# Five rows beside the first decoding, a token shift on two engines, twelve buffers for the first modulation weights

## The chip, the cores and the metric

The kernel runs on one core of one Trainium2 chip. A core has five engines with a queue each: PE (TensorE, matrix products), DVE (VectorE), ACT (ScalarE), POOL (GpSimd) and SP (SyncE, which here only issues transfers). The metric is the device time of one execution in microseconds.

## The reference, cut to what matters

Two layers over 256 context tokens and 256 latent tokens of width 1024. Layer 0 mixes tokens by a bidirectional mLSTM, layer 1 by a bidirectional RWKV-7; behind each stands PEER, which retrieves 128 experts a token (8 heads, the best 16 of 256 candidates each).

```python
for i in range(DEPTH):
    mx = jnp.split((s_lat @ ada_w[i] + ada_b[i])[:, None, :], N_MOD, axis=-1)      # modulation
    mc = jnp.split((s_ctx @ ada_w[i] + ada_b[i])[None, None, :], N_MOD, axis=-1)
    hx = x * (1.0 + mx[1]) + mx[0]
    hc = ctx * (1.0 + mc[1]) + mc[0]
    ...
    x = _layernorm(DN_ALPHA * x + mx[2] * yx, ln_g[i, 0], ln_b[i, 0])
    hx = x * (1.0 + mx[4]) + mx[3]
    ...

# RWKV-7: token shift, then the projections of the six mixes
xm = h[None] + (shifted - h)[None] * mu[:, None, None, :]
r, k, v = jnp.einsum('nbtd,nde->nbte', xm[:3], w_rkv)
... xm[3] -> w1, w2 (decay), xm[4] -> a1, a2, xm[5] -> g1, g2

# PEER: ids of the experts, then a row of u and a row of v for each
u = jnp.take(u_tab, eidx, axis=0)
act = jax.nn.gelu(jnp.einsum('ted,td->te', u, xb), approximate=False)
wgt = gate * act
return jnp.einsum('te,ted->td', wgt, jnp.take(v_tab, eidx, axis=0))
```

## The kernel before, in words

Every fp32 product is made of three TensorE products of a hi and a lo part (`mm3`, L97 to L99). A weight is loaded (`load_raw`, L83 to L90), ScalarE copies it to its hi part (L77), and VectorE, or GpSimd where the caller says so, subtracts that to get the lo part (`split`, L78). TensorE thus waits in turn for a load, for ScalarE and for VectorE. A tile scheduler with a heap of priorities fixes the order of the instructions on every engine's queue when the kernel is built; an instruction that waits holds up all that stands behind it on its engine.

**The start.** `build` opens the weight stream (`open_w`, four raw buffers) and runs `ada_pass` for the first third of layer 0's modulation. It loads 16 tiles of 128 x 1024 from `ada_w`, in eight steps of two (L87), and TensorE multiplies each as it comes (L151). The tiles go into the four buffers of the weight stream, because the pass is called without buffers of its own. Then VectorE adds the bias (L156), TensorE transposes, and the modulation stands in columns. `mlstm` follows: it loads the tokens (`xT`, two transfers of 1 MB at L291, s = 0 for the context and s = 1 for the latents), modulates them in eight blocks (L299 on VectorE for one half, L297 on ScalarE for the other), makes the hi parts on ScalarE (L300) and the lo parts on VectorE (L301), and begins with the products for q and k. The space of `cw`, the weights of the convolution, is the one that the pass held before.

**The RWKV projections.** `rwkv_proj` makes six mixes. `mix(m, seqs)` builds, for each of eight blocks `kt`, a tile `xm` (three buffers) of both sequences or the latents alone: `h * om` (om is 1 − mu), plus the shifted `h` times `mu` (L667, VectorE), a hi part (L669, ScalarE) and a lo part. The first mix (for k) has `first=True`: its mult is on ScalarE (L653) and its lo part on VectorE for three blocks of four. The five others have the mult on VectorE (L655) and the lo part on GpSimd (L670):

```python
for s in seqs:
    if first:
        S.activation(xm[:, s], hk[s][:, kt, :], AF.Copy, scale=om[:, m, kt:kt + 1])
    else:
        V.tensor_scalar(xm[:, s], hk[s][:, kt, :], om[:, m, kt:kt + 1], None, op0=ALU.mult)
...
(V if first and kt % 4 < 3 else G).tensor_tensor(lo[:, kt, :], xf, hi[:, kt, :].bitcast(F32), op=ALU.subtract)
```

In order: k with its mix, the second mix `xw` (for the decay) called behind the second of eight k rows, the mix for r behind the fifth, then `xa`, the eight r rows (`r_ps`), `xv`, and the products for a (`lo_ps`), `xg` and v. The tiles hi and lo of a mix of both sequences have two buffers.

**The first decoding.** `peer_two` computes rows of the expert products (u rows) for 384 of the 512 tokens densely; for the last 128 tokens it gathers single rows by GpSimd (L1588), with a dot product on VectorE for each (L1596). `retrieval` finds the experts and decodes their ids (L1360 to L1370, all on VectorE). While it does, `between` puts work beside it: 12 u rows with lo parts on GpSimd, a modulation pass, and three more u rows into banks b3 to b5 whose results wait until slot C exists (L1631). Then u rows and gathers are interleaved.

## Time and profile before

| | |
|---|---|
| median of 3 runs | 3297.94 us (3294.22 to 3300.07) |
| the profiled execution | 3297.34 us, span of its instructions 3295.5 us |
| mean granted TensorE clock | 0.967 |
| TensorE busy | 3053.1 us, 93% of the span |
| VectorE busy | 2495.4 us, 76% |
| ScalarE busy | 1542.7 us, 47% |
| GpSimd busy | 766.9 us, 23% |

An engine's share is a mean over stages with different limits. It says little of what a change in one stage is worth; for that a stretch is looked at by itself, with the busy time of all engines and with what ended each wait. "Idle before" in a row is the time that the engine stood still ahead of the instruction, and the arrow names what ended it. Times that begin a row are counted from the start of the span.

### The profile page before, as it was taken

What the parts mean: (1) busy time and instruction counts of PE and PEld (TensorE: products, weight loads), DVE (VectorE), ACT (ScalarE), POOL (GpSimd) and SP (SyncE); (2) the same over time, 40 slices, a digit from 0 to 9 for tenths busy, and PEclk for the clock granted to TensorE, in tenths of its full rate; (3) what the DMA queues carried; (4) which work ended last, traced back from release to release, by engine and by line L of the source; (5) the groups of instructions that cost most, each with busy time, mean ns of one, the idle gap of its engine ahead of it and who ended that gap; (6) DMA issues with size and microseconds to landing.
All of it is one profiled execution on the core that took longest, in us unless ns stands there. A gap on an engine that the chain in (4) does not pass through costs nothing.

```text
span 3295.5 us, 54703 instructions
## 1 busy us (share of the span) xinstructions
PE 3053.1 (93%) x20325; PEld 2616.2 (79%) x20325; DVE 2495.4 (76%) x5426; ACT 1542.7 (47%) x2867; POOL 766.9 (23%) x672
## 2 busy tenths in 40 slices
PE   7999999799999899999997897788889999999998
PEld 4776799699988789877874764477879999888887
DVE  5838679767978788899788738996776939887555
ACT  3524343335733333465444447466644443444443
POOL 1110044331033333403342320011306830000000
PEclk8999999999999999999998999789999999999999
DMA  5236542686377788836884248575744554556554
GB/s 209 93 97 201 194 146 83 212 280 222 113 239 274 239 270 287 290 133 233 287 284 148 96 142 248 163 214 159 220 161 151 176 179 155 173 173 223 189 190 147
DMA packets 251883, 633.83 MB, mean 192 GB/s; under 512 B 39840, under 2 KB 97312, under 8 KB 251360
## 3 DMA queue, kind: packets, MB, share of 16 engines
q1 hardware_dynamic: 180672, 478.27, 44.1%
q0 software_dynamic: 37152, 135.28, 12.3%
q10 hardware_dynamic: 33792, 16.78, 1.8%
q8 instruction: 159, 2.61, 0.3%
q14 instruction: 108, 0.88, 0.1%
HBM read 589.06 MB, written 41.19 MB: 191 GB/s over the span
## 4 chain that ended last, share of the span: by engine, by line
PE 68%; DVE 17%; DMA 7%; issue 5%; ACT 2%; POOL 2%; SPq 0%; ACTq 0%; DVEq 0%; POOLq 0%
PE acc L1715 12%; PE acc L1820 11%; PE u_ps L97 7%; PE u_ps L99 7%; PE u_ps L98 7%; PE gp L1673 2%; PE ada_ps L151 2%; DMA unit<-urows,rows 1%; DVE lo_w L78 1%; DVE o_qk L327 1%; DMA raw<-ada_w 1%; DVE eq L1369 1%; DMA unit<-uT 1%; DVE xm L667 1%; PE vo L99 1%
## 5 line engine op out<-in xcount | busy, mean ns | idle before, releaser
L77 ACT ACTIVATE hi_w<-raw 128x1024 fp32r<-128x1024 f32 x339 | 358.1, 1057 | 504.4 <-PE u_ps L98 208.6
L78 DVE TENSOR_TENSOR lo_w<-raw,hi_w 128x1024 fp32r<-128x1024 f32 x281 | 345.8, 1231 | 277.2 <-ACT hi_w L77 277.1
L77 ACT ACTIVATE hi_w<-unit 128x512 fp32r<-128x512 f32 x522 | 326.3, 629 | 488.6 <-PE u_ps L98 263.4
L78 DVE TENSOR_TENSOR lo_w<-unit,hi_w 128x512 fp32r<-128x512 f32 x492 | 335.6, 691 | 150.0 <-ACT hi_w L77 148.6
L99 PE MATMUL u_ps<-hd,lo_w 128*128 128x384 f32 (+1 forms) x1024 | 345.5, 337 | 12.8 <-DVE lo_w L78 7.1
L97 PE MATMUL u_ps<-hd,hi_w 128*128 128x384 f32 (+1 forms) x1024 | 348.3, 340 | 2.1 <-ACT hi_w L77 1.0
L98 PE MATMUL u_ps<-hd,hi_w 128*128 128x384 f32 (+1 forms) x1024 | 344.3, 336 | 0.0
L99 PE MATMUL u_ps<-carry,lo_w 128*128 128x256 f32 x1088 | 307.4, 283 | 6.4 <-POOL lo_w L78 5.9
L97 PE MATMUL u_ps<-carry,hi_w 128*128 128x256 f32 x1088 | 309.1, 284 | 4.4 <-ACT carry L211 4.4
L98 PE MATMUL u_ps<-carry,hi_w 128*128 128x256 f32 x1088 | 307.0, 282 | 0.0
L1715 PE MATMUL acc<-lo_w,wh 128*128 128x512 f32 x718 | 283.7, 395 | 7.5 <-DVE lo_w L78 7.4
L1715 PE MATMUL acc<-hi_w,wh 128*128 128x512 f32 x718 | 282.9, 400 | 6.5 <-ACT hi_w L77 4.3
L1715 PE MATMUL acc<-hi_w,wl 128*128 128x512 f32 x718 | 282.1, 393 | 0.0
L1588 POOL DMA_INDIRECT unit<-vtab,rows x128 | 178.5, 1394 | 363.9 <-DVE xt L1601 181.6
L1588 POOL DMA_INDIRECT unit<-urows,rows x128 | 160.5, 1254 | 421.3 <-DVE unit L1596 271.2
L99 PEld LDWEIGHTS u_ps<-carry,lo_w 128*128 128x128 f32 x1088 | 206.4, 190 | 7.4 <-POOL lo_w L78 6.8
L97 PEld LDWEIGHTS u_ps<-carry,hi_w 128*128 128x128 f32 x1088 | 206.6, 190 | 5.4 <-ACT carry L211 4.8
L99 PEld LDWEIGHTS u_ps<-hd,lo_w 128*128 128x128 f32 x1024 | 195.7, 191 | 17.4 <-DVE lo_w L78 10.7
L98 PEld LDWEIGHTS u_ps<-carry,hi_w 128*128 128x128 f32 x1088 | 206.6, 190 | 0.8 <-DVE carry L212 0.2
L97 PEld LDWEIGHTS u_ps<-hd,hi_w 128*128 128x128 f32 x1024 | 195.9, 191 | 4.5 <-ACT hi_w L77 2.2
L98 PEld LDWEIGHTS u_ps<-hd,hi_w 128*128 128x128 f32 x1024 | 195.7, 191 | 1.1
L1596 DVE SCALAR_TENSOR_TENSOR unit<-unit,xt 128x1024 f32<-128x1024 f32 x128 | 155.0, 1219 | 36.0 <-DMA unit<-urows,rows 35.4
(526 smaller groups left out, 7551.7 us busy)
## 6 DMA issues: line engine op xcount, KB each, us to landing
raw<-vtab SPq DMA_DIRECT2D x144, 512.0 KB
unit<-uT SPq DMA_DIRECT2D x136, 512.0 KB
unit<-vtab SPq DMA_DIRECT2D x128, 512.0 KB
raw<-uT SPq DMA_DIRECT2D x128, 512.0 KB
raw<-ada_w SPq DMA_DIRECT2D x80, 512.0 KB
PK<-dr_pk SPq DMA_DIRECT2D x64, 448.0 KB
raw<-w_qkT SPq DMA_DIRECT2D x16, 512.0 KB
raw<-w_in SPq DMA_DIRECT2D x16, 512.0 KB
```

Source lines behind the costliest of these rows:

```text
L77: nc.scalar.activation(hi, raw, AF.Copy)
L78: (eng or nc.vector).tensor_tensor(lo, raw, hi.bitcast(F32), op=ALU.subtract)
L97: mm(out, lhi, rhi, start=start, stop=False)
L98: mm(out, lhi, rlo, start=False, stop=False)
L99: mm(out, llo, rhi, start=False, stop=stop)
L151: nc.tensor.matmul(ps[32 * g:32 * g + 32, :], E.sc[:, kt, :], raws[g // 2][:, g % 2 * 512:g % 2 * 512 + 512], start=kt == 0, stop=kt == KT ...
L327: V.scalar_tensor_tensor(dst, src, cw[:, ct, k:k + 1], dst, op0=ALU.mult, op1=ALU.add)
L1588: G.indirect_dma_start(out=t, out_offset=None, in_=src, in_offset=bass.IndirectOffsetOnAxis(ap=rows1[:, s:s + 1], axis=0))
L1596: return V.scalar_tensor_tensor(t, t, 1.0, xt, op0=ALU.mult, op1=ALU.mult, accum_out=act[:, s:s + 1])
L1673: mm(gp[:, t], At[t], Bg[:, x, t // 2, :, t % 2], start=x == 0, stop=x == 1)
L1715: mm(accs[2 * tt + n], l[:, ts], r, start=j == 0 and y == 0, stop=j == 127 and y == 2)
L1820: mm(acc[tt * 2 + n], l[:, x, ts], r[:, n * 512:(n + 1) * 512], start=(j + x == 0 and l is wh and r is vhi), stop=(j + x == 127 and l is wl))
```

## The change

Three edits. The first modulation pass gets 12 buffers of its own, in its own pool. In `mix`, the mult is on ScalarE and the lo part on VectorE for every mix. In `between`, five u rows instead of three stand beside the decoding; the two more are in the two banks of `ps_u`, and the rows that are left for later start two further on.

```diff
-        def mix(m, seqs, first=False):
+        def mix(m, seqs):
...
                 for s in seqs:
-                    if first:
-                        S.activation(xm[:, s], hk[s][:, kt, :], AF.Copy, scale=om[:, m, kt:kt + 1])
-                    else:
-                        V.tensor_scalar(xm[:, s], hk[s][:, kt, :], om[:, m, kt:kt + 1], None, op0=ALU.mult)
+                    S.activation(xm[:, s], hk[s][:, kt, :], AF.Copy, scale=om[:, m, kt:kt + 1])
...
                 S.activation(hi[:, kt, :], xf, AF.Copy)
-                (V if first and kt % 4 < 3 else G).tensor_tensor(lo[:, kt, :], xf, hi[:, kt, :].bitcast(F32),
-                                                                 op=ALU.subtract)
+                V.tensor_tensor(lo[:, kt, :], xf, hi[:, kt, :].bitcast(F32), op=ALU.subtract)
...
-        xk = mix(1, (0, 1), True)
+        xk = mix(1, (0, 1))
...
-                for x in range(3):
-                    beside.append((EARLY + LATER + x, ps.tile([128, TD], F32, name="u_ps", tag=f"b{3 + x}", bufs=1)))
-                    u_prod(beside[x][1], halves(load(uT[beside[x][0]]), G))
+                for x in range(5):
+                    up = ps_u.tile([128, TD], F32, name="u_ps") if x > 2 else \
+                        ps.tile([128, TD], F32, name="u_ps", tag=f"b{3 + x}", bufs=1)
+                    beside.append((EARLY + LATER + x, up))
+                    u_prod(up, halves(load(uT[EARLY + LATER + x]), G))
...
-                advance(ada_pass(E, A, 0, 0, m0, pool, ps, "ada", 2), None)
+                advance(ada_pass(E, A, 0, 0, m0, pool, ps, "ada", 2, own=12), None)
```

What the scheduler makes of it is seen at three places. The first is SP at the start of the program (`raw` is a weight tile, `xT_243` holds the context tokens and `xT_244` the latents, `cw` to `bg` are small tables). Before:

```order
L87 DMA raw<-ada_w 128x1024 x4
L291 DMA xT_243<-tokT 128x2048
L141 DMA ada_bt<-ada_b 2x512 x4
L87 DMA raw<-ada_w 128x1024 x12
L85 DMA raw<-w_gP 128x1024
L291 DMA xT_244<-tokT 128x2048
L263 DMA cw<-conv_wT 128x144
L265 DMA cb<-conv_bT 128x16
L267 DMA bq<-b_qkT 128x16
L269 DMA bg<-b_gT 128x1
L85 DMA raw<-w_qkT 128x1024 x4
```

And now:

```order
L87 DMA raw<-ada_w 128x1024 x5
L141 DMA ada_bt<-ada_b 2x512 x4
L87 DMA raw<-ada_w 128x1024 x11
L85 DMA raw<-w_gP 128x1024
L291 DMA xT_243<-tokT 128x2048
L263 DMA cw<-conv_wT 128x144
L265 DMA cb<-conv_bT 128x16
L267 DMA bq<-b_qkT 128x16
L269 DMA bg<-b_gT 128x1
L291 DMA xT_244<-tokT 128x2048
L85 DMA raw<-w_qkT 128x1024 x4
```

Both loads of xT moved behind the weights of the modulation, and xT_244 behind cw and the three small tables.

The second is VectorE where the second mix begins (`carry_18007` and `carry_18008` are the modulated tokens of the context and of the latents). Before:

```order
L670 TENSOR_TENSOR xlo<-xm,xhi 128x512
L667 SCALAR_TENSOR_TENSOR xm<-carry_18008,rmu,xm 128x192
L655 TENSOR_SCALAR xm<-carry_18007,rom 128x256
L655 TENSOR_SCALAR xm<-carry_18008,rom 128x256
L667 SCALAR_TENSOR_TENSOR xm<-carry_18007,rmu,xm 128x255
L667 SCALAR_TENSOR_TENSOR xm<-carry_18008,rmu,xm 128x4x63
```

And now (L664 is the old L667, and L667 the lo part, the old L670):

```order
L667 TENSOR_TENSOR xlo<-xm,xhi 128x512 x2
L664 SCALAR_TENSOR_TENSOR xm<-carry_18008,rmu,xm 128x192
L664 SCALAR_TENSOR_TENSOR xm<-carry_18007,rmu,xm 128x255
L664 SCALAR_TENSOR_TENSOR xm<-carry_18008,rmu,xm 128x4x63
L664 SCALAR_TENSOR_TENSOR xm<-carry_18007,rmu,xm 128x255
L667 TENSOR_TENSOR xlo<-xm,xhi 128x512 x2
```

The mults have left the queue, and a lo part stands in it for each block.

The third is GpSimd at the end of the first decoding (`unit` is the ring of buffers that loads and gathers share, `urows` the table of u rows). Before:

```order
L78 TENSOR_TENSOR lo_w<-unit,hi_w 128x512 x20
L1588 DMA unit<-urows,rows_3194 128x1024 x2
L78 TENSOR_TENSOR lo_w<-unit,hi_w 128x512 x2
L1588 DMA unit<-urows,rows_3194 128x1024
L78 TENSOR_TENSOR lo_w<-unit,hi_w 128x512 x4
L1588 DMA unit<-urows,rows_3194 128x1024 x123
```

And now (L1586 is the old L1588):

```order
L78 TENSOR_TENSOR lo_w<-unit,hi_w 128x512 x20
L1586 DMA unit<-urows,rows_3194 128x1024
L78 TENSOR_TENSOR lo_w<-unit,hi_w 128x512 x2
L1586 DMA unit<-urows,rows_3194 128x1024
L78 TENSOR_TENSOR lo_w<-unit,hi_w 128x512 x4
L1586 DMA unit<-urows,rows_3194 128x1024
L78 TENSOR_TENSOR lo_w<-unit,hi_w 128x512 x4
L1586 DMA unit<-urows,rows_3194 128x1024 x123
```

One gather fewer stands ahead of the first two lo parts, and four lo parts more stand among the first gathers. The order of TensorE is the same at this place.

## Rows read from the trace of the kernel before

**Rows 1.** The page: the chain that ended last, share of the span by engine.

```profile
PE 68%; DVE 17%; DMA 7%; issue 5%; ACT 2%; POOL 2%; SPq 0%; ACTq 0%; DVEq 0%; POOLq 0%
```

**Rows 2.** Busy time by stretch: length, each engine's us (instructions), granted clock, DMA share, GB/s.

```profile
60.00:150.00 90.00, 84.14 (x360) 66.80 (x359) 88.14 (x191) 57.90 (x74) 15.44 (x8) 1.00 0.27 87
...
1782.00:1802.00 20.00, 9.23 (x44) 7.02 (x43) 20.00 (x34) 9.81 (x15) 11.37 (x9) 0.76 0.00 0
1802.00:1841.00 39.00, 39.00 (x184) 32.57 (x184) 20.68 (x35) 15.18 (x26) 7.64 (x9) 0.95 0.30 95
1841.00:1888.00 47.00, 35.56 (x228) 33.13 (x227) 43.94 (x70) 23.95 (x38) 26.14 (x16) 0.89 0.29 91
1888.00:1912.00 24.00, 24.00 (x108) 19.81 (x107) 11.68 (x15) 8.21 (x15) 6.67 (x8) 1.00 0.33 107
```

The engines stand in the order PE, PEld (its weight loads), DVE, ACT, POOL.

**Rows 3.** The chain that ended last, 0 to 60 us: start, us, what.

```profile
1.74 3.68 DMA raw<-ada_w
```

**Rows 4.** TensorE's weight loads, first and fourth tile of ada_w: start, us, what [idle before].

```profile
5.53 0.22 PEld L151 LDWEIGHTS ada_ps<-raw,sc_lhs 128*32 128x32 f32 x4 [5.53 <-issue]
...
9.63 0.19 PEld L151 LDWEIGHTS ada_ps<-raw,sc_lhs 128*32 128x32 f32 x4 [1.10 <-DMA raw<-ada_w]
```

**Rows 5.** Timeline of all engines, end of the modulation pass and start of mlstm.

```profile
32.90 1.05 PE L151 MATMUL ada_ps<-raw,sc_lhs 128*32 128x512 f32 x4 [2.21 <-DMA raw<-ada_w]
...
35.95 0.33 SPq L263 DMA_DIRECT2D cw<-conv_wT  x1
...
37.75 1.85 SPq L85 DMA_DIRECT2D raw<-w_qkT  x4
...
43.80 0.59 ACT L297 ACTIVATE xT<-xT,modsT 128x256 f32<-128x256 f32 x1
...
44.90 0.59 ACT L297 ACTIVATE xT<-xT,modsT 128x256 f32<-128x256 f32 x1
...
46.50 1.04 ACT L77 ACTIVATE hi_w<-raw 128x1024 fp32r<-128x1024 f32 x1
...
48.86 0.50 PE L99 MATMUL qk_ps<-hhi,lo_w 128*128 128x512 f32 x1 [0.15 <-DVE lo_w L78]
```

**Rows 6.** Instructions on the tile xm: ns least/median/most, first and last start, shapes.

```profile
L653 ACT ACTIVATE xm<-carry,rom x16: 491/494/509, 1752.9 to 1780.8; 128x256 f32<-128x256 f32 x16
```

**Rows 7.** Timeline of all engines, first and second mix of the RWKV projections.

```profile
1771.04 1.66 ACT L669 ACTIVATE xhi<-xm 128x512 fp32r<-128x512 f32 x3
...
1773.43 1.89 DVE L670 TENSOR_TENSOR xlo<-xm,xhi 128x512 fp32r<-128x512 f32 x3 [2.17 <-DMA tok<-tk]
1774.16 2.10 ACT L653 ACTIVATE xm<-carry,rom 128x256 f32<-128x256 f32 x5 [1.46 <-DVE xlo L670]
...
1775.24 1.99 DVE L667 SCALAR_TENSOR_TENSOR xm<-carry,rmu,xm 128x255 f32<-128x255 f32 x5
...
1794.04 1.82 DVE L667 SCALAR_TENSOR_TENSOR xm<-carry,rmu,xm 128x255 f32<-128x255 f32 x2
...
1794.33 1.31 POOL L670 TENSOR_TENSOR xlo<-xm,xhi 128x512 fp32r<-128x512 f32 x1 [0.95 <-ACT xhi L669]
...
1801.55 0.80 PE L99 MATMUL k_ps<-xhi,lo_w 128*128 128x512 f32 x1 [5.08 <-DVE lo_w L78]
```

**Rows 8.** Busy time by stretch of L655, of L667, of L670 (DVE, POOL).

```profile
1841.00:1888.00 47.00, 16.15 (x29) 0.89 0.29 91
...
1841.00:1888.00 47.00, 19.12 (x29) 0.89 0.29 91
...
1841.00:1888.00 47.00, 0.00 (x0) 26.14 (x16) 0.89 0.29 91
```

**Rows 9.** Timeline of all engines behind the first decoding.

```profile
619.14 1.21 POOL L1588 DMA_INDIRECT unit<-urows,rows  x1 [32.75 <-PE ada_ps L151]
...
622.95 0.45 PE L99 MATMUL u_ps<-hd,lo_w 128*128 128x384 f32 x1 [2.08 <-POOL lo_w L78]
```

## The prediction

> **What bounds the kernel now.** The share of the chain of waits comes first: TensorE makes 68% of it, VectorE 17%, DMA 7% [rows 1]. So work taken from an engine is worth something only in a stretch where TensorE waits for that engine. A table of busy time by stretch finds these stretches, and the reader is to compare its columns [rows 2]. From 1782 to 1802 us VectorE is busy all of the 20 us and TensorE 9.23; from 1841 to 1888 VectorE is busy 43.94 of 47 us, ScalarE 23.95, TensorE 35.56. Both belong to the RWKV projections. From 1888 on TensorE is busy without a gap, so what is won before comes out at the end. In the mLSTM projections (60 to 150) VectorE is busy 88.14 of 90 us: the change leaves that work alone, but an earlier start moves it whole. Last come the start of the program, where TensorE waits for loads, and the first decoding, where it waits for GpSimd's lo parts.

> **Part A, twelve buffers (start of the program).** Four buffers hold 16 loads of 512 KB. The first lands 3.68 us after its issue [rows 3], and the first four are consumed at 5.53 to 9.63, (9.63 − 5.53) / 3 = 1.37 us apart [rows 4]; later groups wait for TensorE to give a buffer back, and the last matmuls start at 32.90 and last 1.05 us, to 33.95 [rows 5]. With twelve buffers all loads stream: the last lands at 5.53 + 15 × 1.37 = 26.1, its matmuls end at 27.1. That is 6.8 us earlier.

> Not all of it arrives. The order on SP shows both 1-MB loads of xT moved behind the modulation weights, and xT_244 behind cw as well. The issue of cw stands 2.0 us behind the end of the pass today (35.95), because its space is that of the pass, and the load after the four small ones 1.8 later (37.75) [rows 5]. So xT_244 is issued at 27.1 + 3.8 = 30.9 and, as the double of a 512-KB load, lands 3.68 + 1.37 = 5.05 later, at 36.0; today it landed long before it was used. From there ScalarE works through eight blocks. Now a block is one L297 (0.59) and two L300, 1.10 from start to start (43.80 to 44.90) [rows 5]; the L300 of the other half, on xT_243, can be done while xT_244 is under way, and one L300 is (1.10 − 0.59) / 2 = 0.26, so a block takes 0.85 and eight 6.8. The split of the first w_qkT then starts at 42.8 and not at 46.50; from it to the L99 that waits for its lo part are 2.36 us in both. **A: −3.7 us.** Ends: −6.8 if xT_244 lands in time, −1.0 if blocks keep 1.10 (44.8, −1.7) and a little more is lost behind it. I take −3.7, since nothing else stands before the L300 of the first half.

> **Part B, token shift on ScalarE and VectorE.** Prices first. Back to back a mult on ScalarE takes 2.10 / 5 = 0.42, a shifted multiply-add on VectorE 1.99 / 5 = 0.40, a lo part on VectorE 1.89 / 3 = 0.63 [rows 7]. The median of a mult on ScalarE, alone or in a row, is 0.494 [rows 6]. The pair of multiply-adds that runs beside a GpSimd lo part takes 1.82 us (1794.04, beside 1794.33) instead of 2 × 0.40 = 0.80: each lo part on GpSimd takes 1.0 us from VectorE, more than the 0.63 that VectorE needs to do it itself [rows 7].

> Second mix (1782 to 1802): VectorE is the bound, and TensorE gets its lo part only at 1801.55, after 5.08 us of waiting [rows 7]. Afterwards ScalarE is the bound: its 9.81 us [rows 2] and 16 mults × 0.42 = 6.7 make 16.5, VectorE needs 16 × 0.40 + 8 × 0.63 = 11.4 beside it. The 16.5 hold the copy of a ninth block, and copies that run on without a wait are shorter than those in the table; about 1 us of it can go. With the last lo part of a weight behind it (1.2) that is 16.5 us from 1781.9: 1798.4 and not 1801.55. **−3.2.**

> The r rows with the mixes xa and xv (1841 to 1888): 29 mults leave VectorE (16.15 us), 19.12 us of multiply-adds become 29 × 0.40 = 11.6, and 16 lo parts come from GpSimd (26.14 us there) at 0.63 = 10.1 [rows 8]. VectorE: 43.94 − 16.15 − 7.5 + 10.1 = 30.4. ScalarE: 23.95 + 29 × 0.42 = 36.1, or 38.3 at the median of 0.494. TensorE needs 35.56 or less. ScalarE has most, on the mean 37.2, and I add 1.8 for the hand-over to VectorE and back to TensorE at the end (two multiply-adds, a lo part, some start): 39.0 instead of 47. **−8.0.** The mixes for k and r lie beside a TensorE that is busy (1802 to 1841) or, for xg, in the full stretch from 1888 [rows 2]: nothing. **B: −11.2**, ends −4 (three xm buffers give half the overlap) and −15.4 (36.1 without hand-over, and the second mix bound by VectorE's 11.4).

> [...]

> **Part C, five rows beside the first decoding.** The order of TensorE does not change: these rows stand behind the transposes of the decoding in both kernels, so they fill no gap. What moves is on GpSimd: the first gather starts at 619.14 and takes 1.21 us, a second follows, then the first lo parts, for which TensorE waits 2.08 us until 622.95 [rows 9]. Now the second gather stands behind these lo parts: about −1.0, since it is no longer than the first. In return four more lo parts (some 1.3 us each by 1794.33 [rows 7], as they have the same number of elements) stand before the gathers, which come up to 6 us later; VectorE's dots and SP's loads wait for those. **C: −1.0**, ends −1.3 and +2.

> **Sum.** −3.7 − 11.2 − 1.0 = −15.9. The profiled execution took 3297.34 us, 0.6 under the median of the runs shown, so the sum is made on either: 3297.34 − 15.9 = **3281.4**.

> **Rivals.** (1) Half of B: blocks wait for each other through three xm buffers, since each goes ScalarE, VectorE, ScalarE, VectorE; for it speaks that two of these steps are now on the fullest engine. B −5.6: 3287. (2) A comes to nothing, because xT_244 lands later than worked out, behind the rest of the queue: 3285. (3) Everything at its good end: −6, −15, −1.3 give 3275. (4) The other side: **ScalarE and VectorE work in turns.** If no two blocks overlap, a block costs 2 × 0.42 + 2 × 0.40 + 0.55 + 0.63 = 2.82 us (0.55 a copy back to back, 1.66 / 3 [rows 7]). The r rows hold 14.5 such blocks: 14.5 × 2.82 and the 14.3 us of ScalarE's other work (23.95 less 16 copies at 0.6) are 55.2, 8.2 more than 47; the second mix comes to 8 × 2.82 + 4.1 + 1.2 = 27.9 against 19.7, 8.2 more. With A and C that is 3309. By these sums B becomes a loss from 2.1 us a block, and the whole change slower by 0.2% from 2.6. Today's eight blocks of the second mix take 2.3 each ((19.7 − 1.2) / 8) with VectorE full; against the rival speak the buffers and ScalarE's idle time, of which the table shows 23 us. (5) The change does not do what it says, in that both ends are set by something else, a load for instance: 3296.

> **How the numbers follow.** The forecast .52 (its own range 3277 to 3286), rival 1 .20, rival 2 .07, rival 3 .11, rival 4 .05, rival 5 .05. The range goes from all good ends at once (3273.8) less two us for TensorE's clock, whose grant is 0.76 and 0.89 of full in the two stretches of B, between its two levels, after waits that become shorter [rows 2], to rival 1 with C's bad end and a little of A's, 3291: 3272 to 3291; rivals 4 and 5 are left out, and about as much at the edges. A measurement of this kernel can tell about 0.2% (6.6 us) from no change: under 3291.3 are the forecast and rivals 1 to 3 less some tail, .86; rival 5 and tails are the same, .09; rival 4 and its mild form .05.

> **What will show it.** A: the last L151 ends near 27, xT_244 is issued near 31, the first L99 of qk_ps near 45. If that L99 comes with 42, xT was no hindrance; if at 48, the blocks were. B: the L99 of k_ps that waits until 1801.55 comes 16.5 us behind the start of its mix and not 19.7, GpSimd is empty, VectorE at about 30 and ScalarE near 37 in the r rows, which last 39. If a block of the mix takes over 2.1 us, rival 4 is right. C: the first L99 behind the decoding a microsecond earlier after the first gather, and no new waits of TensorE from 623 to 700. The forecast is wrong if the stage behind a gain gives it back, most of all the VectorE-bound mLSTM projections or the gathers.

## The result and the profile after

The changed kernel takes 3283.93 us (median of 11 runs, 3277.94 to 3290.82), the kernel before 3300.07 in the same 11 rounds (3294.22 to 3309.1): a ratio of 0.995, 95% interval 0.994 to 0.996. That is 16.1 us less; 15.9 was forecast. The forecast time was 3281.4, the range 3272 to 3291. The profiled execution took 3284.95 us (span 3283.1), a little over its median, and that of before, 3297.34, a little under its own; so the two profiles differ by 12.4 us and not by 16.

The sum came out as forecast, its terms did not. Two were worth as much as forecast or more, and one cost 5 to 7 us where a gain of 1 was expected. The sections below follow the three.

**The start.** Timeline of the changed kernel (start, length, engine, line, what, idle time before and what ended it), the answer to [rows 4, 5]:

```profile
25.37 0.14 PEld L151 LDWEIGHTS ada_ps<-raw,sc_lhs 128*32 128x32 f32 x4 [1.07 <-DMA raw<-ada_w]
...
29.76 0.44 SPq L291 DMA_DIRECT2D xT<-tokT  x1
...
35.00 1.08 ACT L297 ACTIVATE xT<-xT,modsT 128x256 f32<-128x256 f32 x2
...
36.60 1.08 ACT L297 ACTIVATE xT<-xT,modsT 128x256 f32<-128x256 f32 x2
...
41.39 1.04 ACT L77 ACTIVATE hi_w<-raw 128x1024 fp32r<-128x1024 f32 x1
...
44.05 0.39 PE L99 MATMUL qk_ps<-hhi,lo_w 128*128 128x512 f32 x1
```

The last of the 16 modulation weights is consumed at 25.37 and not at 32.90. The load of xT_244 is issued at 29.76, ScalarE begins its blocks at 35.00, takes 1.60 for two, and the L99 that stood at 48.86 comes at 44.05. A microsecond of these 4.8 is the one profile of before: in the five profiles of kernels without the twelve buffers this L99 starts at 47.50 to 48.86 (mean 48.06), in the eight with them at 43.59 to 44.92 (mean 44.21), so the buffers bring 3.8 us there.

**The RWKV projections.** Busy time of the changed kernel by stretch, laid at the same steps as the stretches of [rows 2] (second mix; r rows; a and v products). After the length stand the busy time of PE, PEld, DVE, ACT and POOL, then the granted clock, DMA share and GB/s:

```profile
1782.00:1798.00 16.00, 8.36 (x39) 6.40 (x38) 12.50 (x26) 14.68 (x30) 0.00 (x0) 0.77 0.00 0
...
1837.00:1873.00 36.00, 31.72 (x225) 30.29 (x224) 31.22 (x57) 33.67 (x66) 0.00 (x0) 0.91 0.35 116
1873.00:1897.00 24.00, 24.00 (x109) 19.89 (x108) 10.57 (x19) 10.52 (x20) 0.00 (x0) 1.00 0.34 112
```

The r rows last 36 us instead of 47. ScalarE is busy 33.67 of them, VectorE 31.22 instead of 43.94, GpSimd not at all. The 36 us fall into a front part, in which ScalarE has no gap, and a rest, in which TensorE has none; between them lies TensorE's only wait (us in total, times, longest):

```profile
1837.00:1850.00 13.00, 8.72 (x55) 7.62 (x54) 10.03 (x22) 12.94 (x26) 0.00 (x0) 0.95 0.12 40
1850.00:1856.00 6.00, 6.00 (x30) 5.67 (x28) 5.93 (x10) 4.85 (x10) 0.00 (x0) 0.53 0.54 170
1856.00:1873.00 17.00, 17.00 (x144) 17.00 (x144) 15.26 (x25) 15.88 (x31) 0.00 (x0) 1.00 0.46 155
...
PE rt_ps L720 <- DVE nr L711: 4.3, 1, 4.3
```

`nr` holds the inverse norms of the keys, made on VectorE and ScalarE in turn; its step on ScalarE (L709) stands on the queue behind the copies and mults of the mix. Instructions on the tile xm of the changed kernel (ns least/median/most, first and last start), beside [rows 6]:

```profile
L652 ACT ACTIVATE xm<-carry,rom x80: 492/496/522, 1752.6 to 1878.4; 128x256 f32<-128x256 f32 x80
L664 DVE SCALAR_TENSOR_TENSOR xm<-carry,rmu,xm x80: 409/475/487, 1753.1 to 1878.9; 128x255 f32<-128x255 f32 x32, 128x252 f32<-128x252 f32 x24, 128x192 f32<-128x192 f32 x24
L667 DVE TENSOR_TENSOR xlo<-xm,xhi x32: 680/686/693, 1773.4 to 1870.2; 128x512 fp32r<-128x512 f32 x32
```

No multiply-add takes over 487 ns any more; in [rows 7] a pair of them took 1.82 us beside GpSimd. And the L99 of the third k row, which waited until 1801.55, starts at 1797.14; what TensorE now waits for there is a weight's hi part, which ScalarE makes:

```profile
1795.88 0.80 PE L97 MATMUL k_ps<-xhi,hi_w 128*128 128x512 f32 x1 [7.16 <-ACT hi_w L77]
...
1797.14 0.80 PE L99 MATMUL k_ps<-xhi,lo_w 128*128 128x512 f32 x1
```

**The first decoding and what follows.** GpSimd and TensorE of the changed kernel, the answer to [rows 9]:

```profile
617.04 1.21 POOL L1586 DMA_INDIRECT unit<-urows,rows  x1 [30.94 <-PE ada_ps L151]
618.28 2.51 POOL L78 TENSOR_TENSOR lo_w<-unit,hi_w 128x512 fp32r<-128x512 f32 x2
...
619.61 0.44 PE L99 MATMUL u_ps<-hd,lo_w 128*128 128x384 f32 x1 [1.09 <-POOL lo_w L78]
```

TensorE waits 1.09 us instead of 2.08: the forecast microsecond. But the first dot product, at 634.49 before, comes at 641.04:

```profile
641.04 1.22 DVE L1594 SCALAR_TENSOR_TENSOR unit<-unit,xt 128x1024 f32<-128x1024 f32 x1
```

and 125 us later there is a loss that no line of the prediction has. Busy time of TensorE alone by stretch, behind it the granted clock, DMA share and GB/s. Before:

```profile
760.00:770.00 10.00, 9.92 (x89) 1.00 0.92 317
770.00:780.00 10.00, 8.97 (x58) 0.76 1.01 394
780.00:790.00 10.00, 10.00 (x61) 0.73 0.76 271
790.00:800.00 10.00, 10.00 (x111) 1.00 0.25 77
```

After:

```profile
760.00:770.00 10.00, 8.02 (x58) 0.84 0.97 365
770.00:780.00 10.00, 10.00 (x49) 0.50 0.84 278
780.00:790.00 10.00, 10.00 (x45) 0.50 0.75 249
790.00:800.00 10.00, 10.00 (x96) 0.97 0.34 116
```

In 760 to 800 us TensorE made 319 products before (89, 58, 61 and 111) and makes 248 now, and for 20 of the 40 us its granted clock is 0.50, the lower of the two levels that both traces show (taken from 750 to 800 us in steps of half a microsecond, 98 of 100 read 1.00 or 0.50 in each). Ahead of that stand a load that comes late and a wait of TensorE behind it:

```profile
766.05 0.63 ACT L77 ACTIVATE hi_w<-unit 128x512 fp32r<-128x512 f32 x1 [4.59 <-DMA unit<-uT]
...
766.89 0.47 PE L97 MATMUL u_ps<-hd,hi_w 128*128 128x128 f32 x1 [1.98 <-ACT slotA L1532]
```

The bank that TensorE waits for is emptied by ScalarE (L1532), which stands right behind that hi part. These are the short u rows: the last eight of `u_rest`, for 128 tokens only, a load of 512 KB each. Loads and gathers share the buffers of the ring, and from 700 to 800 us SP waits 58.5 us for one that a lo part gives back and 26.6 us for one that a dot product gives back.

Where the time went is best seen by laying the same product of TensorE in both traces side by side, all 20,325 of them, and taking the difference of their starts (after less before):

| at (us of the kernel before) | difference | since |
|---|---|---|
| 49, first L99 of qk_ps | −4.8 | the start |
| 420, end of the mLSTM layer | −5.0 | |
| 430 | −2.6 | first products for the queries |
| 757 | −1.8 | the decoding |
| 774 to 788, end of the short rows | +5.1 | **+7 in the short rows** |
| 1505 | +1.6 | |
| 1772, first k row | +0.4 | |
| 1806, third k row | −4.0 | second mix |
| 1887, end of the r rows | −14.2 | r rows |
| 1956 | −14.9 | |
| 2060 | −12.5 | RWKV front |
| end | −11.9 | |

So in this pair of profiles the token shift alone brings the time; what the twelve buffers win is given back, half of it at 430 us and the rest in the short rows. The step at 430 is a wait of TensorE for a lo part on GpSimd, 1.99 us instead of 1.27, with 3.4 us of half clock behind it. It is not the buffers' doing: the kernel of experiment 3 that moves the lo parts alone, without the buffers, has it too. Changed kernel, before, lo parts alone:

```profile
421.89 0.48 PE L99 MATMUL q_ps<-hd,lo_q 128*128 128x256 f32 x1 [1.99 <-POOL lo_q L78]
426.02 0.39 PE L99 MATMUL q_ps<-hd,lo_q 128*128 128x256 f32 x1 [1.27 <-POOL lo_q L78]
426.16 0.39 PE L99 MATMUL q_ps<-hd,lo_q 128*128 128x256 f32 x1 [1.94 <-POOL lo_q L78]
```

### The profile page after: what moved, and what is told of

Its sections match the earlier page's. It is cut to its first block, busy times and chain, and to the rows that moved or that the text cites. A ratio compares the mean times of both kernels' runs of the same rounds, so it can differ in the third digit from the quotient of the medians.

```text
span 3283.1 us, 54682 instructions
## 1 busy us (share of the span) xinstructions
PE 3056.0 (93%) x20325; PEld 2623.9 (80%) x20325; DVE 2463.1 (75%) x5400; ACT 1567.6 (48%) x2931; POOL 721.4 (22%) x634
## 3 DMA queue, kind: packets, MB, share of 16 engines
q0 software_dynamic: 37152, 135.28, 12.4%
## 5 line engine op out<-in xcount | busy, mean ns | idle before, releaser
L77 ACT ACTIVATE hi_w<-raw 128x1024 fp32r<-128x1024 f32 x339 | 358.1, 1057 | 493.8 <-PE u_ps L98 212.5
L77 ACT ACTIVATE hi_w<-unit 128x512 fp32r<-128x512 f32 x522 | 326.7, 630 | 492.1 <-PE u_ps L98 277.7
L99 PE MATMUL u_ps<-hd,lo_w 128*128 128x384 f32 (+1 forms) x1024 | 349.6, 341 | 12.2 <-DVE lo_w L78 7.9
L97 PE MATMUL u_ps<-hd,hi_w 128*128 128x384 f32 (+1 forms) x1024 | 352.2, 344 | 4.3 <-ACT hi_w L77 2.3
L98 PE MATMUL u_ps<-hd,hi_w 128*128 128x384 f32 (+1 forms) x1024 | 348.4, 340 | 0.0
L99 PE MATMUL u_ps<-carry,lo_w 128*128 128x256 f32 x1088 | 307.7, 283 | 6.4 <-POOL lo_w L78 5.9
L1586 POOL DMA_INDIRECT unit<-vtab,rows x128 | 179.3, 1401 | 362.9 <-DVE xt L1599 173.9
L1586 POOL DMA_INDIRECT unit<-urows,rows x128 | 155.9, 1218 | 419.6 <-DVE unit L1594 291.5
L99 PEld LDWEIGHTS u_ps<-hd,lo_w 128*128 128x128 f32 x1024 | 199.6, 195 | 16.8 <-DVE lo_w L78 11.2
L99 PEld LDWEIGHTS u_ps<-carry,lo_w 128*128 128x128 f32 x1088 | 206.7, 190 | 7.4 <-POOL lo_w L78 6.7
L97 PEld LDWEIGHTS u_ps<-hd,hi_w 128*128 128x128 f32 x1024 | 200.0, 195 | 6.1 <-ACT hi_w L77 2.9
L98 PEld LDWEIGHTS u_ps<-hd,hi_w 128*128 128x128 f32 x1024 | 199.7, 195 | 1.0
```

The costliest lines, as they stand in the source:

```text
L77: nc.scalar.activation(hi, raw, AF.Copy)
L97: mm(out, lhi, rhi, start=start, stop=False)
L98: mm(out, lhi, rlo, start=False, stop=False)
L99: mm(out, llo, rhi, start=False, stop=stop)
L1586: G.indirect_dma_start(out=t, out_offset=None, in_=src, in_offset=bass.IndirectOffsetOnAxis(ap=rows1[:, s:s + 1], axis=0))
```

## The experiments

Each kernel is timed against the kernel before in the same rounds. The time of one kernel spreads over 8 to 18 us from run to run, so intervals are ±4 to ±7 us wide (0.12 to 0.21%), and single effects of under 4 us are read from the traces by stage.

**1. Each edit alone.** The theory read from the two traces: A −5, B −12 to −15, C +2 to +7. Rival: the terms of the prediction.

Twelve buffers alone:

```diff
-                advance(ada_pass(E, A, 0, 0, m0, pool, ps, "ada", 2), None)
+                advance(ada_pass(E, A, 0, 0, m0, pool, ps, "ada", 2, own=12), None)
```

> Twelve buffers alone. Theory 1 (read from the trace of the changed kernel: its mlstm products start 4.9 us earlier and keep that to 420 us): -5 us at the first L99 of qk_ps, and -3 to -5 at the end, ratio 0.9985 to 0.999. Rival (what TensorE wins at the start is taken back by the VectorE-bound stage or the first decoding): under 1 us at the end, ratio 1.000.

Measured: ratio 0.9978 (0.9966 to 0.999), −7.3 us (−11 to −3). In the trace the first L99 of qk_ps stands at 43.78, 5.1 us earlier than before, and the offset at 420 us is −5. So the gain is real and passes through the VectorE-bound mLSTM stage. In this one profile it is gone by the end (+1.6): from 628 us on the offset is +0.4, behind the step at 430 us and a stretch in which TensorE stood at half clock 7 us longer than before. Such differences come and go between the profiles. The theory's −3 to −5 lies in the interval; the rival, under 1 us, does not.

Token shift alone (the two hunks of `mix`):

> Token shift on ScalarE and VectorE alone. Theory 1 (the trace of the changed kernel: offset -0.1 us at the start of the k rows, -15.0 at the end of the v products, of which 3 come back behind them): -12 to -15, ratio 0.9955 to 0.9965. Rival (the prediction's term): -11.2, ratio 0.9966. Rival that ScalarE is the bound: over 2.1 us a block and no gain.

Measured: 0.9947 (0.993 to 0.9964), −17.4 us (−23 to −12). By stage: from the first k product to the first L99 of the third k row 25.4 us instead of 29.8, from the last k product to the a products 38.4 instead of 48.4: 14.4 in these two. Both stages repeat within about 3 us in the kernels that hold the whole edit (24.0 to 27.2, and 37.1 to 38.4), and in those that hold none of it (29.1 to 29.9, and 48.4 to 50.3). The theory's 12 to 15 is right; the prediction's 11.2 is too small and lies just outside the interval.

Five rows alone:

> Five rows beside the first decoding alone. Theory 1 (in the changed kernel the offset goes from -3 to +5 us between 615 and 775 us, since gathers start later and TensorE then has a wait of 2 us and stands at half clock for 13.7 us more): +2 to +7, ratio 1.0006 to 1.002. Rival 1 (the prediction's term): -1.0, ratio 0.9997. Rival 2 (the longer half clock is chance, not the edit's): within 1 us of before.

Measured: 1.0007 (0.9995 to 1.0019), +2.4 us (−1.7 to +6.3). By time alone that is not clear of nothing. By stage it is: the offset goes from −1.7 at 624 us to +5.5 at 786, and TensorE in the short rows has nearly the same picture as with all three edits:

```profile
760.00:770.00 10.00, 7.84 (x59) 0.88 0.95 359
770.00:780.00 10.00, 10.00 (x49) 0.50 0.83 284
780.00:790.00 10.00, 10.00 (x45) 0.50 0.72 249
790.00:800.00 10.00, 10.00 (x94) 0.92 0.32 107
```

In the ten profiles that keep the short rows at the end they take 26 to 29 us without the five rows (26.5, 26.4, 27.9, 28.1, 27.0, 29.3) and 33 to 35 with them (33.3, 33.3, 33.3, 34.5), the clock being at half for 10 to 17 us without and 24 to 31 with. Rival 2, chance, falls.

**2. The first two edits without the third.**

> Twelve buffers and the token shift, three rows beside the decoding as before. Theory 1 (the third edit costs): -17 to -20, ratio 0.994, 3 to 6 us faster than all three edits. Rival 1 (the third edit is worth -1.0): -15, slower than all three by 1. Rival 2 (chance): as all three, -16.

Measured: 0.9944 (0.9926 to 0.9962), −18.5 us. Its profiled execution is 3278.42 us against 3284.95 with all three, the offset behind the short rows −3.2 instead of +5. Between the medians (0.9944 and 0.995) the timing can't tell; the stage can.

**3. Which half of the token shift counts.** The first kernel moves only the mults to ScalarE, the second only the lo parts to VectorE:

```diff
# first
-                    if first: ...
-                    else:
-                        V.tensor_scalar(xm[:, s], hk[s][:, kt, :], om[:, m, kt:kt + 1], None, op0=ALU.mult)
+                    S.activation(xm[:, s], hk[s][:, kt, :], AF.Copy, scale=om[:, m, kt:kt + 1])
# second
-                (V if first and kt % 4 < 3 else G).tensor_tensor(lo[:, kt, :], xf, ...
+                V.tensor_tensor(lo[:, kt, :], xf, ...
```

> Only the mults to ScalarE, lo parts of the five mixes stay on GpSimd. If VectorE's 16 us of mults are what counts (VectorE then has about 28 of the 47 us of the r rows, ScalarE 34 is the bound): -10 to -14, nearly all of the gain. If what GpSimd takes from VectorE counts (1.0 us for each lo part): -4 to -7, half of it.

> Only the lo parts to VectorE, mults stay there. By the prices of the rows VectorE goes from 43.9 to about 40 us in the r rows and from 19.7 to 16.9 in the second mix: -5 to -6, ratio 0.998. If contention is not the cause of the long multiply-adds: VectorE gets 10 us more work, +4 to +8.

Measured: mults alone 0.9984 (0.9971 to 0.9998), −5.3 us; lo parts alone 0.9978 (0.9964 to 0.9991), −7.3 us. From the last k product to the last product of v the kernel before takes 109.0 us, the whole edit 98.8, mults alone 102.3, lo parts alone 108.8. The second mix takes 27.8 and 28.2 us instead of 29.8 (25.4 with the whole edit). So the mults alone are worth 5 us of 17 by time and 8.7 of 14.6 by stage: within the 4 to 7 that the theory of contention gave by time, and not nearly all.

With the mults alone GpSimd still works beside VectorE. Groups of VectorE's instructions in its r rows (busy us, mean ns of one, idle before):

```profile
L664 DVE SCALAR_TENSOR_TENSOR xm<-carry,rmu,xm 128x255 f32<-128x255 f32 x13 | 11.1, 856 | 2.9 <-ACT xm L652 2.9
L664 DVE SCALAR_TENSOR_TENSOR xm<-carry,rmu,xm 128x192 f32<-128x192 f32 x8 | 6.0, 752 | 1.6 <-ACT xm L652 1.6
```

and with the lo parts alone:

```profile
L655 DVE TENSOR_SCALAR xm<-carry,rom 128x256 f32<-128x256 f32 x34 | 10.6, 346 | 0.0
L670 DVE TENSOR_TENSOR xlo<-xm,xhi 128x512 fp32r<-128x512 f32 x16 | 10.5, 685 | 0.9 <-ACT xhi L669 0.9
L667 DVE SCALAR_TENSOR_TENSOR xm<-carry,rmu,xm 128x255 f32<-128x255 f32 x13 | 6.2, 476 | 0.0
```

A multiply-add takes 856 ns beside GpSimd and 476 without it. The kernel with the mults alone differs from the whole edit only in the engine of the lo parts, and with the whole edit no multiply-add takes over 487 ns. So GpSimd's lo parts are the cause of the long ones, as the prediction had it. The mult is longer beside GpSimd as well, with a mean of 589 ns in the r rows of the kernel before and 346 without GpSimd. By what way GpSimd lengthens them, no run here shows. But where the mults stay on VectorE, its work is only put later. From the last k product to the a products it is 35.9 us instead of 48.4, and then the products for a wait 2.3 us and those for v 4.0 us for a lo part of a weight.

```profile
PE rv L98 <- DVE lo_w L78: 4.0, 1, 4.0
PE lo_ps L99 <- DVE lo_w L78: 2.3, 1, 2.3
```

That the lo parts alone are faster by time (−12 to −3 us) and gain only some 2 us in these stages of their one profile (1.6 in the second mix, 0.2 here) is not explained. Its profiled execution, with a span of 3308.4 us, was the slowest of its twelve.

**4. What makes the five rows cost.** Two candidates: the lo parts on GpSimd among the first gathers, or that the 44 gathers are spread over 35 rows instead of 37, so that more of them meet the short rows. The first kernel gives the two added rows their lo parts on VectorE, the second moves two gathers to the next stages:

```diff
# first
+                    u_prod(up, halves(load(uT[EARLY + LATER + x]), (None if x > 2 else G)))
# second
-    GS = (44, 4, 144, 2, 44, 18)
+    GS = (42, 4, 146, 2, 44, 18)
```

> All three edits, the lo parts of the two added rows on VectorE instead of GpSimd, so that the four lo parts no longer stand among the first gathers. Theory 1 (the ratio of gathers to rows decides): wait of 4 to 5 us at 766 us and 24 us of half clock as with all three, ratio 0.995. Rival (late gathers decide): first dot product 6 us earlier, no long wait at 766 us, ratio 0.993.

> All three edits, and two of the 44 gathers that are interleaved with the remaining u rows moved to a later stage (42 and 146 instead of 44 and 144). Theory 1 (with two long rows fewer beside them, more of the 44 gathers meet the eight short rows at the end, each of which wants 512 KB in 1.4 us; loads come late, TensorE waits 2 us at 767 us and then stands at half clock for 24 us): the wait for unit<-uT before it falls from 4.6 us to under 3, the half clock to 10 to 17 us, the offset gains 4 to 7 us by 790 us; ratio 0.993. Rival (the gathers are late because lo parts stand before them on GpSimd): no change there, ratio 0.995.

Measured: 0.9944 (0.9924 to 0.9965) with the lo parts on VectorE, 0.9971 (0.9958 to 0.9984) with two gathers fewer. The short rows take 33.3 us in the first and 34.5 in the second, with 24 and 31 us at half clock: neither candidate is the cause. (A short row at full clock takes 2.7 us, 21.6 for the eight in experiment 5, and not the 1.4 of the second expectation.) In the first the gathers are as late as with all three edits, although no lo part stands in front of them on GpSimd. The fourth starts at 637.74 (637.88 with all three edits, 631.32 before). With all three edits it follows the last added lo part on GpSimd; in this kernel it waits until that same lo part, now on VectorE, gives back a buffer of the ring that loads and gathers share. All three edits, then this kernel:

```profile
637.88 0.95 POOL L1586 DMA_INDIRECT unit<-urows,rows  x1 [0.27 <-POOL lo_w L78]
...
636.77 0.69 DVE L78 TENSOR_TENSOR lo_w<-unit,hi_w 128x512 fp32r<-128x512 f32 x1 [1.34 <-ACT hi_w L77]
637.74 0.94 POOL L1586 DMA_INDIRECT unit<-urows,rows  x1 [6.66 <-DVE lo_w L78]
```

The two rows more take buffers of the ring ahead of the gathers, whichever engine makes their lo parts. That the late gathers are in turn what makes the loads of the short rows late, 125 us on, is not shown: no kernel here has five rows and early gathers. The second kernel also loses later: its offset goes from +6 at 788 us to +13 at 1400, as two gathers more stand in a stage that has no room for them.

**5. The short rows elsewhere.** If the cost is that TensorE waits for loads in eight short rows in a row, each of which is 24 products with a load of their own, it should go when they no longer stand together at the end. One behind every third long row, without and with the third edit; and, in a third kernel, all eight ahead of the long rows:

```diff
-        u_rest = itertools.chain(u_rows(EARLY + LATER + len(beside), NA), u_rows(0, EARLY, T))
+        def spread(a, b, n):
+            for k, _ in enumerate(a, 1):
+                yield
+                if k % n == 0 and next(b, 0) is None:
+                    yield
+            for _ in b:
+                yield
+        u_rest = spread(u_rows(EARLY + LATER + len(beside), NA), u_rows(0, EARLY, T), 3)
# third kernel
+        u_rest = itertools.chain(u_rows(0, EARLY, T), u_rows(EARLY + LATER + len(beside), NA))
```

> Twelve buffers and the token shift, three rows beside the decoding, and the eight short rows (128 tokens wide) spread among the long ones, one behind every third, instead of all at the end. Theory 1 (TensorE waits for loads in the short rows and its clock falls to half until they are over: 26 to 29 us for them without the third edit, of which 20 would do at full clock): 5 to 7 us less by 790 us than with the two edits, no half clock there, ratio 0.992 to 0.993. Rival (the loads bound that whole stage, wherever the short rows stand): no change, ratio 0.9944.

> All three edits, and the short rows spread in the same way. Theory 1 (what the third edit costs, 33 us for the short rows instead of 26 to 29, comes of their standing in a row at the end): the cost is gone, within 1.5 us of the kernel before this one, ratio 0.992 to 0.993. Rival (later gathers cost wherever the short rows stand): 5 us slower than that one, ratio 0.994 to 0.995.

> Twelve buffers and the token shift, three rows beside the decoding, and the eight short rows ahead of the long ones. If only the gathers' traffic at the end makes their loads late: 5 to 7 us less, as with spread rows. If short rows in a row keep the half clock wherever they stand (TensorE comes from the decoding at half clock, 14 us of it at 600 us): 26 us or more for them at half clock, 0.21 us for each of 192 products, and no gain or a loss of up to 8 us, ratio 0.994 to 0.997.

Measured: 3271.55 us, 0.9914 (0.9893 to 0.9934) spread without the third edit; 3273.47 us, 0.9918 (0.9901 to 0.9935) spread with it; 3279.94 us, 0.9934 (0.9918 to 0.995) ahead of the long rows. TensorE where the short rows ended before, in the kernel spread with all three edits:

```profile
760.00:770.00 10.00, 10.00 (x65) 1.00 0.84 276
770.00:780.00 10.00, 10.00 (x73) 1.00 0.92 328
780.00:790.00 10.00, 10.00 (x110) 1.00 0.29 88
```

The full clock holds throughout. By 790 us the offset is −7.8 without the third edit and −9.7 with it. From 640 to 790 us it falls by 6.7 in the one and by 6.6 in the other, so the third edit costs nothing any more; with the short rows at the end it rises there by 2.4 without the third edit and by 6.9 with it. The same eight rows ahead of the long ones have an offset of −10.0 at 790 and no half clock in between either. So it is neither the short rows as such nor their standing in a row that brings the clock down: with waits of 0.3 to 2.0 us among them it falls, and in these three kernels, where no wait among them is over 0.1 us, it does not. By time, spread rows (0.9914) and rows ahead (0.9934) can't be told from the two edits alone (0.9944); by stage they can. Spread rows with the third edit (0.9918) can be told from the changed kernel (0.995) by time too. The kernel spread without the third edit beats both kernels, by 31 us in the medians the one before (22 to 35 by its interval) and by about 12 the changed one, whose ratio of 0.995 was taken in other rounds.

## Why the prediction was right, and where only its sum was

**What bounds the kernel** was read rightly: the stretches in which VectorE was full and TensorE waited are those in which time was won, and behind 1888 us the gain was passed on.

**A (forecast −3.7).** Right. Last matmuls to the end: 26.4 (27.1 forecast). Issue of xT_244: 29.76 (30.9). Start of ScalarE's blocks: 35.00 (36.0). A block: 0.80 (0.85). Start of the weight's hi part: 41.39 (42.8). Each step came about a microsecond early, and the L99 4.8 us earlier instead of 3.7. But the kernels without the buffers have that microsecond too: over all profiles the L99 comes 3.8 us earlier, which is the forecast. Alone the edit is worth 7.3 ± 4 us.

**B (forecast −11.2).** Contention (in experiment 3 a multiply-add of 856 ns beside GpSimd and of 476 without it), a chain that overlaps and, in the second mix, ScalarE as the new bound were right. VectorE's sum was right as well (30.4 forecast, 31.22 measured). In the r rows ScalarE bounds only the front: it is busy 12.94 of the first 13 us and holds back nr, for which TensorE waits 4.28 us, and then TensorE works 23 us without a gap, 6 of them at a granted clock of 0.53. The prediction let ScalarE's sum and a hand-over make up the whole stretch, and 39 for 36 came near by luck. That sum, 23.95 + 29 × 0.42 = 36.1 up to 38.3, was also mis-sized: ScalarE was busy 33.67. A microsecond of the difference is the copy of one weight (L77), of which this stretch holds 8 and the one of before 9. For the rest, instructions of ScalarE overlapped by 0.10 us where one followed another without a wait. In the chain of the changed kernel a copy and the mult behind it start 0.52 and 0.40 us apart:

```profile
1793.96 0.52 ACT xhi L666
1794.48 0.40 ACT xm L652
```

where the table of the tile has medians of 0.621 and 0.496, 0.10 us more each. The prediction used the short time for what it added (0.42) and the long one for what was there, in the 23.95 us that ScalarE had spent with waits between its instructions. The second mix brought 4.4 in the stage with the edit alone (29.8 less 25.4) and 4.8 in the changed kernel (25.0), instead of 3.2; ScalarE was busy 14.68 of 16 us there, where 16.5 were summed. By itself the mult is dearer on ScalarE: 0.496 us there, and 0.346 on VectorE without GpSimd (experiment 3). In the r rows of before, beside GpSimd, it took VectorE 16.15 / 29 = 0.56 us, so there it was not. The good end of −15.4 is worked out only in part: the r rows without the hand-over give 47 − 36.1 = 10.9, and no line gives the 4.5 that are left for the second mix.

**C (forecast −1.0, ends −1.3 and +2).** The step that failed is the bound on what late gathers cost. The microsecond ahead of the first L99 came (1.09 for 2.08), and the prediction saw that the gathers would come up to 6 us later (6.5). It named lo parts on GpSimd as the reason. They do stand in front of the fourth gather, but experiment 4 shows that it is as late without them, for want of a buffer of the ring. And it let the third edit cost at most 2 us, looking for new waits only from 623 to 700 us, where there are none. The wait of TensorE comes at 766 and is in fact 1.98 us, but behind it the clock was granted at half for 24 us, over the rest of the short rows: 5 to 7 us. The prediction counted the clock in the stretches of B and did not look at this one, where the trace of before already shows 0.76 and 0.73.

**The sum.** −15.9 forecast, −16.1 measured: by stage, A and B were together 3 to 4 us better than forecast and C about 7 worse, which would give −12 to −13, as the pair of profiles has it (−12.4). By time the edits alone add up to −7.3 − 17.4 + 2.4 = −22, with ±5 on each of the first two, so that the three together can't be told from their sum. That the forecast sum fits to 0.2 us is luck: it holds two errors of opposite sign, and the measured difference has an interval of ±3 us.

**The rivals.** Half of B: no, blocks overlap, 1.3 us of ScalarE each. A to nothing: not for the lateness of xT_244, though in single profiles as much as A's gain is lost before the RWKV layer, by waits and half clock that kernels without the buffers have too. ScalarE and VectorE in turns, and so slower: no, ScalarE was busy 33.67 of 36 us.

**Open.** Why the five rows make the loads of the short rows later: the engine of the lo parts and the ratio of gathers to rows are ruled out, and how the ring's buffers fall to loads and gathers was not tried. Why the wait for a lo part at 420 to 430 us is 1.9 to 2.0 us in some profiles (the changed kernel, A alone, lo parts alone) and under 1.3 in others (before, A and B). And what the lo parts alone win where.

## What to carry to other kernels

Price an edit by what it takes from its neighbours too: moving the lo parts off GpSimd to a VectorE that was already full made its other instructions faster here, since a lo part on GpSimd had stretched two multiply-adds by a microsecond (1.82 us for the pair beside it in the second mix, 0.80 for two in a row). The stages gained little by it (1.8 us) while the mults were still on VectorE, and 5.9 us once they had left. Put short pieces of work that each need a whole load where loads have room, among long pieces, and not behind them; here that was worth 9 us by stage without the third edit and 13 with it. And where a change makes something later, look along the queue for the next place in which TensorE can be left waiting, and read the granted clock there: here the wait was 1.98 us, and 5 to 7 were lost.
